# A decoder step on one core: other marks for splitting the next weights, one block's V first, three small steps moved

## The chip, the cores and the metric

The kernel runs on one core of one Trainium2 chip. The metric is the device time of one execution in microseconds (us); of the kernel before, three runs gave 1424.87 to 1428.22 us with a median of 1428.19. Every engine (TensorE, here PE; VectorE, DVE; ScalarE, ACT; GpSimd, POOL; SyncE, SP, which issues the DMAs) works through its own list of instructions in order, and the lists are tied by semaphores.

## The reference

One inference step of a hybrid decoder for 1024 prompt tokens and 8 x 8 sample tokens, 1088 tokens in all, in float32:

```python
u = rmsnorm(x)                                   # 1088 x 1024
a, q, k, v, g_a, g_b = split(u @ w_in)           # a 512, q/k/v 768 each, gates 1024 each
A = pool(a) @ w_pa                               # trailing means over 2/4/8/16 tokens
B = attention(q, k, v) @ w_pb                    # 3 head groups of 4 heads of 64; dilation 1, 4, 16
h = x + (sigmoid(g_a) * A + sigmoid(g_b) * B) @ w_o
y = h + relu(rmsnorm(h) @ w_up)**2 @ w_down      # 1024 -> 4096 -> 1024
```

q and k are RMS-normed per head. The sample tokens attend to cached keys and values as well; the caches go out shifted by eight rows.

## The kernel before

Every float32 operand of a large product is split into a high half in the type fp32r (a copy on ACT) and a low half (a subtraction on DVE), and a product is three passes: high x high, high x low, low x high. `split` (line 113) is this pair; in the trace it is lines 114 (ACT) and 115 (DVE), and lines 1279 and 1280 are the same pair in `put`. PE runs in the order of the program. On the other engines a planner, which simulates the program's timeline when it is built, sets the order. `behind_pe` makes an instruction wait until a given matmul is done.

The stages, by the trace: pooling input and row norms (to 58 us), three head groups of attention (g = 2, 1, 0, to about 395 us; the gate products begin there), gates, the two branches and `w_o` (to 741 us), the feed-forward's up product and down product.

In a head group the tokens are nine blocks: eight of 128 prompt tokens and block 8, the 64 sample tokens. Blocks 8 and 0 are done together, then 1 to 5 alone, then 6 and 7 together in groups 2 and 1. Where blocks go together, or alone at the end of group 0, the projections run as Q, K, V with 256 columns each (`qkv_part`, line 606; 24 matmuls); blocks 1 to 5 do Q and K as one product of 512 columns and V after it. After a projection the ACT squares (642), DVE `ms` (645), POOL `mr` (646) and ACT scale (651) bring Q and K to unit RMS. Block 8's two halves are first added on DVE (627, 628). A projection's result lies in one of four PSUM banks that are used in turn (`bank`), so the fifth projection after another needs that one's bank free again.

`step()` runs once for each projection (twice for the wide one). It advances every unfinished generator by one: the attention of older blocks (`attend`: transposes at 666, scores 683, row maxima 692, exp 693, transposes 702 and their copies 705, values 716, output copies 723 and 726), the pooling branch, the token sums (`token_sums`, lines 525 to 534: per step some DVE additions and products into one buffer `ts`, then its store to `ts_d`), and the sample tokens' attention (`sample_shared_keys`). `soon` puts a function into a list from which each step runs one. `own_step` advances the sample tokens' attention over their own long cache (pieces `pck` and `pcv`, multiplied on POOL at 855 and 879, reduced on DVE).

Weights of the next group: `line_up` (142) lists the twelve quarters (512 columns, which is two of the eight features panels) of the next Q, K and V weights, each with a key. They go to the places of the present Q, K and V weights. `feed` (157) splits the first of the list as soon as its key's matmul has been issued in the program, and ties the ACT half behind that matmul. The raw quarters come over three buffers (`raw`, DMAs at line 130): a quarter's load is issued when the quarter three ahead of it has been split.

The order inside one product: `gemm` (189) with `by_k=2` goes feature by feature, with all three passes of a feature panel before the next; otherwise a whole pass goes over all eight panels.

Later, in the feed-forward, `norm_sums` (1645) adds the squares of the second half of the rows with matmuls, POOL takes the power (`hr`, 1652), `norm_spread` (1655) builds diagonals on DVE (`dg`, 1657) and spreads them over partitions with four matmuls (`bc`, 1661), and `make_versions` scales the rows (1664) and forms the sums and differences which the later up products use. The up products are units of 24 matmuls; `then` hangs these functions behind chosen units.

At the switch to group 1 the pooling's memory is given back and the tiles of the new group are laid into it. `wT` (a tile of zeros to be filled later, 1142) and `osm` (1145, 1146) are cleared there.

Of the kernel before, what the change touches and what calls it, by code (L numbers as in the profile page):

```python
# [36 lines left out]
def decoder_step(ctx, tc, i, o):  # L37
# [79 lines left out]

    def split_on_vector(dst_hi, dst_lo, src):
        ins = v_.tensor_copy(dst_hi, src)
        v_.tensor_tensor(dst_lo, src, dst_hi.bitcast(F32), op=ALU.subtract)  # L120
        return ins

    def fetch(src, name, a, tied=False):
# [32 lines left out]

    def feed(splitter=split):
        while coming_up and coming_up[0]["key"] in ends_of:
            p = coming_up.pop(0)
            cs = slice(p["a"], p["a"] + 512)  # L160
            ins = splitter(p["wt"][:, 0, cs], p["wt"][:, 1, cs], p["raw"])
# [31 lines left out]

    def gemm(out, n_k, lhs, rhs, by_k=False, middle=None):

        if by_k == 2:
            terms = [(a, b, k) for k in range(n_k) for a, b in PASSES]
        elif by_k:
            terms = [(1, 0, k) for k in range(n_k)] + [(0, b, k) for k in range(n_k) for b in range(2)]
        else:  # L200
            terms = [(a, b, k) for a, b in PASSES for k in range(n_k)]
        for j, (a, b, k) in enumerate(terms):
            last_mm[0] = t_.matmul(out, lhs(a, k), rhs(b, k), start=(j == 0), stop=(j == len(terms) - 1))  # L203
            if middle and j == len(terms) // 2 - 1:
                middle()


# [397 lines left out]

    def qkv_part(g, wts, blk, name, tiles, js, middle=None):

# [13 lines left out]
        if blk == 8:  # L621
            for k in range(KD):
                t_.matmul(pt[:, :N], smp_t[:, k, :], rhs(0, k), start=(k == 0), stop=(k == KD - 1))
                if k < KD - 1:
                    for kk in ((0, 1) if k == 0 else (k + 1,)):
                        last_mm[0] = t_.matmul(pt[:n, :N], smp_t[:, kk, :NS], rhs(1, kk), start=False, stop=False)
            v_.tensor_copy(vt[:n], pt[n:, :256])
            v_.tensor_tensor(pt[:n, :256], pt[:n, :256], vt[:n], op=ALU.add)
        else:
            gemm(pt[:n, :N], KD, lambda s, k: block_cols(g, blk, s, k), rhs, g == 0 and (2 if blk == 0 and js == [2] else 1), middle)  # L630
        for j in js:
# [491 lines left out]
    for g in (2, 1, 0):  # L1123
        nq = i["qk_norm"]
        if g == 1:
# [15 lines left out]
            wT = ap2.tile([P, 2 * P], F32R, name="wT")  # L1141
            v_.tensor_scalar(wT, ident.unsqueeze(1).to_broadcast([P, 2, P]), 0.0, None, op0=ALU.mult)

            for a in range(2):
                v_.memset(osm[64:, a], 0.0)
                v_.memset(osm[64:, a, :, 64], -NEG)
            qs = sp1.tile([P, 768], F32, name="qs")
# [14 lines left out]
        for blks in ((8, 0), (1,), (2,), (3,), (4,), (5,)) + (((6, 7),) if g else ((6,), (7,))):  # L1162

            if g and 6 in blks:
                next_wts = [(place[0] + j) % 3 for j in range(3)]
                for j, after in enumerate((((7, 0), (6, 1), (6, 1), (7, 1)), ((7, 1), (6, 2), (6, 2), (6, 2)), ((7, 2),) * 4)):
                    keys_of = [(g,) + a for a in after]
                    if g == 1 and j == 2:
                        keys_of[3] = (0, 0, "mid")
                    line_up(i["w_in"][2 + 3 * j + g - 1], f"qkv{g - 1}_{j}", *keys_of)  # L1170
            elif not g and 3 in blks:
                wg_first = line_up(lambda a: gate_quarter(a // 512 % 2, a // 1024), "ga0",
                                   *((0, 7, j) for j in (0, 0, 1, 1)), width=2048)
            tiles = {b: qkv_tiles(f"{g}_{b}", b == 8) for b in blks}

            for js in (((0, 1), (2,)) if blks[0] in (1, 2, 3, 4, 5) else ((0,), (1,), (2,))):
                for b in (blks[::-1] if g == 0 and js == (2,) else blks):

# [7 lines left out]

                    def last_quarter():
                        ends_of[0, 0, "mid"] = last_mm[0]
                        feed(split_on_vector)

# [4 lines left out]
                    wide = len(js) == 2  # L1195
                    qkv_part(g, wts, b, f"{g}_{b}", tiles[b], js, middle if wide else last_quarter if (g, b, js) == (0, 0, (1,)) else None)
                    feed()
# [12 lines left out]
                    if 2 in js:  # L1210
                        (sample_block if b == 8 else prompt_block)(g, b, *tiles[b])
                if g == 2 and 2 in js and 8 in blks:
                    start(pool_branch(), "p", now=True)
                    start(token_sums(), "t", now=True)

# [695 lines left out]
    for f in range(0, FIRST, 2):  # L1911
        for n in (0, 2):
            for ff in (f, f + 1):
                groups[ff][n]()
                if f == 0:
                    then({(0, 0): lambda: norm_sums(1), (0, 1): lambda: (norm_spread(1), make_versions())}.get((n, ff), lambda: None))
    for f in range(NG):
# [260 lines left out]
```

## Time and profile before

| | |
|---|---|
| median of three runs | 1428.19 us (1424.87 to 1428.22) |
| profiled execution, its own time | 1423.59 us |
| its span, first to last instruction | 1421.8 us |
| PE busy | 1405.0 us, 99% of the span |
| DVE, ACT, POOL busy | 974.3, 755.7, 227.1 us |
| TensorE clock granted | 1.000 |

A stretch of the span is read by the busy time of each engine in it; a row of the order of time has the start, the length, the engine, the line, the operation, the tiles written and read, and in brackets the idle time before it with what ended that idle time. A row can stand for several like instructions (xcount).

### The profile page before, as it was taken

The page shows a single profiled execution, that of the slowest core. Times are in us where ns is not written, and L with a number is a line of the kernel's source. Part 1 is how long each engine was busy: PE and PEld are TensorE (multiplying, and loading weights), DVE is VectorE, ACT ScalarE, POOL GpSimd, SP SyncE. Part 2 cuts the span into 40 slices and gives each one's busy share as a digit, 9 for nine tenths or more (in the row PEclk, how much of TensorE's full clock was granted, in tenths as well). Part 3 has the DMA queues.
Part 4 walks back from the last instruction along what each step waited for, and adds up shares of the span by engine and source line. Part 5 has one row for each costly group of instructions (what it writes and reads, how often), then busy time and mean ns, then how long its engine had stood idle before and what let it go on. Part 6 is the DMA issues. An engine that isn't in the chain of part 4 may idle for free.

```text
span 1421.8 us, 29482 instructions
## 1 busy us (share of the span) xinstructions
PE 1405.0 (99%) x11101; PEld 1352.6 (95%) x11101; DVE 974.3 (69%) x1806; ACT 755.7 (53%) x1961; POOL 227.1 (16%) x291
## 2 busy tenths in 40 slices
PE   9999999999999999999999999999999999999998
PEld 8988877877999999999999999999999999999998
DVE  7688775786676776875468678765665686664565
ACT  8556755777765223563336455454554544444443
POOL 1721165565500000000000000000000000000100
PEclk9999999999999999999999999999999999999999
DMA  6323789756477777975468768856658987777674
GB/s 212 115 80 109 204 222 213 201 130 145 108 248 232 253 227 234 322 232 165 141 198 272 230 220 255 270 190 223 231 194 278 333 274 258 223 242 226 199 264 168
DMA packets 184543, 303.59 MB, mean 214 GB/s; under 512 B 26568, under 2 KB 90510, under 8 KB 182351
## 3 DMA queue, kind: packets, MB, share of 16 engines
q1 hardware_dynamic: 181326, 258.04, 58.4%
q0 software_dynamic: 3072, 43.65, 9.6%
q8 instruction: 87, 1.43, 0.4%
q14 instruction: 58, 0.47, 0.1%
HBM read 231.55 MB, written 113.73 MB: 243 GB/s over the span
## 4 chain that ended last, share of the span: by engine, by line
PE 93%; DMA 2%; ACT 2%; DVE 1%; POOL 1%; issue 0%; SPq 0%; DVEq 0%; POOLq 0%; ACTq 0%
PE pz L1272 24%; PE pd L2036 24%; PE pg L1272 12%; PE ph L203 7%; PE pqk L203 5%; PE pab L1578 5%; PE pv L203 4%; PE a L329 3%; PE pq L203 1%; PE pk L203 1%; POOL pcv L879 1%; DMA pcv<-in_cache_kv_dram 1%; PE pl L508 1%; DMA wq<-in_qk_norm_dram 0%; DMA keys<-in_kT_dram 0%; PE pog1b L716 0%
## 5 line engine op out<-in xcount | busy, mean ns | idle before, releaser
L2036 PE MATMUL pd<-places 128*128 128x272 f32 x2688 | 334.7, 287 | 0.0
L2036 PEld LDWEIGHTS pd<-places 128*128 128x128 f32 x2688 | 334.6, 188 | 0.0
L1279 ACT ACTIVATE places<-raw_d 128x544 fp32r<-128x544 f32 (+1 forms) x176 | 111.1, 647 | 163.5 <-DMA raw_d<-z_d 61.1
L1280 DVE TENSOR_TENSOR places<-raw_d,places 128x544 fp32r<-128x544 f32 (+1 forms) x176 | 122.6, 711 | 94.8 <-ACT places L1279 92.8
L2076 POOL DMA_DIRECT2D out_kv_sample_dram<-in_cache_kv_dram x96 | 47.1, 490 | 801.3 <-ACT places L1279 586.2
L1272 PE MATMUL pz<-act,places 128*128 128x272 f32 x1080 | 141.5, 289 | 0.0
L1272 PEld LDWEIGHTS pz<-act,places 128*128 128x128 f32 x1080 | 138.2, 188 | 0.0
L203 PE MATMUL ph<-act,places 128*128 128x272 f32 x768 | 97.0, 288 | 0.0
L203 PEld LDWEIGHTS ph<-act,places 128*128 128x128 f32 x768 | 96.5, 188 | 0.1
L1272 PE MATMUL pg<-act,places 128*128 128x272 f32 x576 | 76.6, 290 | 0.0
L1272 PEld LDWEIGHTS pg<-act,places 128*128 128x128 f32 x576 | 73.6, 189 | 0.6 <-issue 0.3
L646 POOL TENSOR_TENSOR mr<-ms,mhalf 128x4 f32<-128x4 f32 (+2 forms) x39 | 56.2, 1443 | 105.6 <-DVE ms L645 104.5
L1272 PE MATMUL pz<-places,apart 128*128 128x272 f32 x528 | 68.2, 287 | 0.0
L1272 PEld LDWEIGHTS pz<-places,apart 128*128 128x128 f32 x528 | 66.8, 188 | 0.0
L203 PE MATMUL pqk<-places,act 128*128 128x512 f32 x240 | 61.0, 403 | 0.7 <-ACT qk L651 0.7
L1272 PE MATMUL pz<-act,apart 128*128 128x272 f32 x456 | 59.7, 289 | 0.0
L1272 PEld LDWEIGHTS pz<-act,apart 128*128 128x128 f32 x456 | 58.3, 188 | 0.1
L203 PEld LDWEIGHTS pqk<-places,act 128*128 128x128 f32 x240 | 44.6, 192 | 10.8 <-ACT qk L651 0.9
L855 POOL TENSOR_TENSOR pck<-pck,qs 128x256 f32<-128x256 f32 x64 | 48.3, 784 | 41.2 <-DMA pck<-in_cache_kv_dram 26.8
L329 PE MATMUL a<-act,places 128*128 128x384 f32 (+1 forms) x288 | 50.3, 332 | 1.4 <-ACT act L307 1.2
L329 PEld LDWEIGHTS a<-act,places 128*128 128x128 f32 x288 | 47.5, 188 | 3.2 <-ACT act L307 1.8
L1578 PE MATMUL pab<-ab,places 128*128 128x272 f32 x384 | 50.5, 287 | 0.0
(433 smaller groups left out, 2836.1 us busy)
## 6 DMA issues: line engine op xcount, KB each, us to landing
out_kv_sample_dram<-in_cache_kv_dram POOLq DMA_DIRECT2D x72, 480.0 KB, 4.8
raw_d<-z_d SPq DMA_DIRECT2D x112, 272.0 KB
z_d<-t SPq DMA_DIRECT2D x80, 272.0 KB
raw_d<-in_w_down_dram SPq DMA_DIRECT2D x80, 256.0 KB
raw_u<-in_w_up_dram SPq DMA_DIRECT2D x64, 256.0 KB
raw_qkv<-in_w_in_dram SPq DMA_DIRECT2D x36, 256.0 KB
pck<-in_cache_kv_dram SPq DMA_DIRECT2D x32, 256.0 KB
pcv<-in_cache_kv_dram SPq DMA_DIRECT2D x32, 256.0 KB
```

What stands on the lines that cost most here:

```text
L203: last_mm[0] = t_.matmul(out, lhs(a, k), rhs(b, k), start=(j == 0), stop=(j == len(terms) - 1))
L329: last_mm[0] = t_.matmul(pts[m][:, :n], wt[:, a, kk, m * P:(m + 1) * P], act4[b][kk][:, :, part4(c)], start=(p == 0 and kk == 0), stop=(p ...
L508: t_.matmul(pl[:, :npr], lin[:, g, :], dp_[:, c0:c0 + npr], start=True, stop=True)
L646: g_.tensor_tensor(r[:n, :H], ms[:n, :H], mhalf[:n, :H], op=ALU.pow)
L855: behind_pe(g_.tensor_tensor(t[:, n], t[:, n], qs[:, :256], op=ALU.mult))
L879: behind_pe(g_.tensor_tensor(tv, tv, sc[:, j + n, :].unsqueeze(2).to_broadcast([P, 4, HD]), op=ALU.mult))
L1272: last_mm[0] = t_.matmul(x[c][:, :Q], A[:, a, k * P:(k + 1) * P], Bv(b, k, c), start=(first and n == 0), stop=(n == len(terms) - 1), skip_ ...
L1279: ins = s_.activation(view(t[:, 0]), src, AF.Copy)
L1280: v_.tensor_tensor(view(t[:, 1]), src, view(t[:, 0]).bitcast(F32), op=ALU.subtract)
L1578: last_mm[0] = t_.matmul(q[x][:, c, :Q], w.rearrange("p s n -> p (s n)")[:, at:at + P], rhs, start=(n == 0), stop=(n == len(terms) - 1))
L2036: last_mm[0] = t_.matmul(chain[t][:, c, :Q], A[:, a, t * P:(t + 1) * P], Z[:, b, c * Q:(c + 1) * Q], start=(fresh and f == 0 and n == 0), ...
L2076: ins = g_.dma_start(d, a)
```

## The change

Five parts.

1. `gemm` takes a function `quarter` and calls it after every six matmuls. In groups 2 and 1, blocks 6 and 7, Q, K and V go feature by feature (`by_k=2`), and after each six matmuls (two feature panels) a key is set and `feed` is run. The next Q's quarters are now keyed to the middle and the end of block 7's Q and the middle and the end of block 6's K; the next K's to the middle and end of block 7's K and of block 6's V; the next V's first three to the first, second and third six matmuls of block 7's V, and its last to the end of the sample block's K in the next group.
2. `split_on_vector`, which split the last quarter of group 0's V on DVE alone behind the middle of block 0's K, is gone.
3. In group 1, too, V of block 0 goes ahead of V of block 8, and V of block 0 goes feature by feature in every group.
4. In group 2 the token sums start after K of blocks 8 and 0 (before: after V). The pooling branch starts where it did.
5. The clearings of `wT` and `osm` go into the list of `soon`, behind eight empty entries, and the one of `wT` waits for PE's latest matmul. `norm_spread` and `make_versions` hang behind the third up unit instead of the second.

```diff
+            if quarter and j % 6 == 5:
+                quarter(j // 6)
...
-            gemm(pt[:n, :N], KD, lambda s, k: block_cols(g, blk, s, k), rhs, g == 0 and (2 if blk == 0 and js == [2] else 1), middle)
+            by_k = 2 if quarter or blk == 0 and js == [2] else g == 0
+            gemm(pt[:n, :N], KD, lambda s, k: block_cols(g, blk, s, k), rhs, by_k, middle, quarter)
...
-            v_.tensor_scalar(wT, ident.unsqueeze(1).to_broadcast([P, 2, P]), 0.0, None, op0=ALU.mult)
-
-            for a in range(2):
-                v_.memset(osm[64:, a], 0.0)
-                v_.memset(osm[64:, a, :, 64], -NEG)
+
+            def clear():
+                behind_pe(v_.tensor_scalar(wT, ident.unsqueeze(1).to_broadcast([P, 2, P]), 0.0, None, op0=ALU.mult))
+                for a in range(2):
+                    v_.memset(osm[64:, a], 0.0)
+                    v_.memset(osm[64:, a, :, 64], -NEG)
+
+            soon(*[lambda: None] * 8, clear)
...
-                for j, after in enumerate((((7, 0), (6, 1), (6, 1), (7, 1)), ((7, 1), (6, 2), (6, 2), (6, 2)), ((7, 2),) * 4)):
-                    keys_of = [(g,) + a for a in after]
-                    if g == 1 and j == 2:
-                        keys_of[3] = (0, 0, "mid")
+                for j, after in enumerate((((7, 0, 1), (7, 0, 3), (6, 1, 1), (6, 1, 3)), ((7, 1, 1), (7, 1, 3), (6, 2, 1), (6, 2, 3)),
+                                           ((7, 2, 0), (7, 2, 1), (7, 2, 2)))):
+                    keys_of = [(g,) + a for a in after] + [(g - 1, 8, 1)] * (j == 2)
...
-                for b in (blks[::-1] if g == 0 and js == (2,) else blks):
+                for b in (blks[::-1] if g < 2 and js == (2,) and 8 in blks else blks):
...
-                    def last_quarter():
-                        ends_of[0, 0, "mid"] = last_mm[0]
-                        feed(split_on_vector)
+                    def quarter(q):
+                        ends_of[g, b, js[0], q] = last_mm[0]
+                        feed()
...
-                    qkv_part(g, wts, b, f"{g}_{b}", tiles[b], js, middle if wide else last_quarter if (g, b, js) == (0, 0, (1,)) else None)
+                    qkv_part(g, wts, b, f"{g}_{b}", tiles[b], js, middle if wide else None,
+                             quarter if g and b in (6, 7) else None)
...
-                if g == 2 and 2 in js and 8 in blks:
-                    start(pool_branch(), "p", now=True)
-                    start(token_sums(), "t", now=True)
+                if g == 2 and 8 in blks and js != (0,):
+                    start(*((pool_branch(), "p") if 2 in js else (token_sums(), "t")), now=True)
...
-                    then({(0, 0): lambda: norm_sums(1), (0, 1): lambda: (norm_spread(1), make_versions())}.get((n, ff), lambda: None))
+                    then({(0, 0): lambda: norm_sums(1), (2, 0): lambda: (norm_spread(1), make_versions())}.get((n, ff), lambda: None))
```

More of the change, by code (lines that the diff above doesn't have):

```diff
@@ L116, in split @@
         return ins
[L118 to L121, printed above, removed]
     def fetch(src, name, a, tied=False):
@@ L155, in line_up, with feed @@
         return wt
-    def feed(splitter=split):
+    def feed():
         while coming_up and coming_up[0]["key"] in ends_of:
@@ L160, in feed @@
             cs = slice(p["a"], p["a"] + 512)
-            ins = splitter(p["wt"][:, 0, cs], p["wt"][:, 1, cs], p["raw"])
+            ins = split(p["wt"][:, 0, cs], p["wt"][:, 1, cs], p["raw"])
             behind_pe(ins, ends_of[p["key"]])
@@ L192, in behind_pe, with gemm @@
                           mybir.DependencyInfo(mybir.DependencyClass.Sync, mybir.DependencyReason.DATA), reason="pace")
-    def gemm(out, n_k, lhs, rhs, by_k=False, middle=None):
+    def gemm(out, n_k, lhs, rhs, by_k=False, middle=None, quarter=None):
         if by_k == 2:
@@ L604, in in_order, with qkv_part @@
                 nat[s, k], nat[s, k + 1] = t[:, 0, :], t[:, 1, :]
-    def qkv_part(g, wts, blk, name, tiles, js, middle=None):
+    def qkv_part(g, wts, blk, name, tiles, js, middle=None, quarter=None):
         n = min(P, TOK - blk * P)
```

## The prediction

> **What bounds the kernel now.** I read the page first, then a table by stretches, then the order of time of PE, and of the engine that released it, at each place where PE stood still.
>
> ```profile
> span 1421.8 us, 29482 instructions
> PE 1405.0 (99%) x11101; PEld 1352.6 (95%) x11101; DVE 974.3 (69%) x1806; ACT 755.7 (53%) x1961; POOL 227.1 (16%) x291
> ```
>
> PE is the bound, and the change neither adds nor removes a matmul. So it can only win what PE stands idle, 1421.8 - 1405.0 = 16.8 us, or add to it. The table by stretches (us, busy time of PE, PEld, DVE, ACT, POOL, clock, DMA share, GB/s) says where that is:
>
> ```profile
> 160.00:190.00 30.00, 25.60 (x189) 22.02 (x188) 21.91 (x75) 18.51 (x87) 9.78 (x12) 1.00 1.02 275
> 190.00:275.00 85.00, 85.00 (x759) 68.50 (x758) 57.29 (x164) 52.51 (x262) 51.40 (x61) 1.00 0.85 206
> 275.00:303.00 28.00, 25.32 (x207) 22.52 (x206) 25.32 (x54) 22.05 (x95) 17.66 (x20) 1.00 0.66 152
> 740.00:755.00 15.00, 13.23 (x104) 12.85 (x103) 8.35 (x14) 4.89 (x9) 2.98 (x5) 1.00 0.63 190
> ```
>
> 4.40 us are lost at the switch from group 2 to 1, 2.68 at the switch from 1 to 0 and 1.77 at the second norm: 8.85 of the 16.8 us. Between the switches PE loses nothing (85.00 of 85.00). The clock is 1.00 in every row. In PE's order of time the losses are these (the bracket is the idle time and its releaser):
>
> ```profile
> 173.58 0.39 PE L623 MATMUL pv<-places,smp_t 128*128 128x256 f32 x1 [1.86 <-ACT qk L651]
> ...
> 180.84 3.06 PE L203 MATMUL pqk<-places,act 128*128 128x512 f32 x12 [0.66 <-ACT qk L651]
> ...
> 186.02 0.65 PE L716 MATMUL pog2b<-pTg2b,v 128*64 128x128 f32 x6 [1.76 <-ACT pTg2b L705]
> ...
> 281.16 1.09 PE L716 MATMUL pog1b<-pTg1b,v 128*64 128x128 f32 x14 [0.25 <-ACT pTg1b L705]
> ...
> 291.43 0.38 PE L203 MATMUL pv<-places,natt 128*128 128x256 f32 x1 [0.86 <-DVE places L119]
> 292.52 0.86 PE L203 MATMUL pv<-places,natt 128*128 128x256 f32 x5 [0.70 <-DVE places L120]
> ...
> 301.00 0.65 PE L716 MATMUL pog1b<-pTg1b,v 128*64 128x128 f32 x6 [0.87 <-ACT pTg1b L705]
> ...
> 750.35 1.16 PE L1661 MATMUL bc<-dg,ones 128*128 128x272 f32 x4 [1.77 <-DVE dg L1657]
> ```
>
> Call them A, B, C (first switch), D, E (two rows, 1.56), F (second switch), G: 1.86 + 0.66 + 1.76 + 0.25 + 1.56 + 0.87 + 1.77 = 8.73 us. That is the most that the seven can return.
>
> **The change part by part.** First switch, the engines behind A to C:
>
> ```profile
> 172.10 0.63 ACT L114 ACTIVATE places<-raw_qkv 128x512 fp32r<-128x512 f32 x1 [1.42 <-DMA raw_qkv<-in_w_in_dram]
> 172.63 0.89 ACT L651 ACTIVATE qk<-pq,mr 64x64 f32<-64x64 f32 x4
> ...
> 179.88 0.91 ACT L651 ACTIVATE qk<-pk,mr 64x64 f32<-64x64 f32 x4 [2.16 <-POOL mr L646]
> 183.31 0.40 ACT L693 ACTIVATE smg2b<-smg2b,sta 128x128 f32<-128x128 f32 x1 [2.53 <-DVE sta L692]
> ```
> ```profile
> 163.00 1.36 DVE L525 TENSOR_TENSOR ts<-act,act 128x544 f32<-128x544 f32 x2 [1.08 <-DMA ts_d<-ts]
> ...
> 170.07 0.21 DVE L645 TENSOR_SCALAR ms<-ms,xeps 64x4 f32<-64x4 f32 x1
> 170.19 0.42 DVE L533 TENSOR_TENSOR ts<-ts 128x272 f32<-128x272 f32 x1
> ...
> 179.12 0.66 DVE L1142 TENSOR_SCALAR wT<-cst 128x256 fp32r<-128x256 f32 x1 [2.97 <-DMA ts_d<-ts]
> 179.88 0.56 DVE L1145 MEMSET osm<- 64x264 f32 x2
> ```
> ```profile
> 170.36 2.10 POOL L646 TENSOR_TENSOR mr<-ms,mhalf 64x4 f32<-64x4 f32 x2 [14.99 <-DVE ms L645]
> 176.76 2.13 POOL L855 TENSOR_TENSOR pck<-pck,qs 128x256 f32<-128x256 f32 x3 [4.30 <-DMA pck<-in_cache_kv_dram]
> 178.85 1.00 POOL L646 TENSOR_TENSOR mr<-ms,mhalf 64x4 f32<-64x4 f32 x1
> ```
>
> *A* is no wait for weights. PE needs the bank that block 8's Q still holds; its scale (172.63) stands on ACT behind the last quarter of V, which waited 1.42 us for its load, and its power was done only at about 171.4, since DVE gave `ms` at 170.07, between the last token sums (163.00 to 170.6). Part 4 takes the sums two projections earlier (2 x 24 matmuls at 0.12, some 6 us). Part 1 frees places up to one projection sooner, some 3 us, so that the loads, which queue in a stretch whose DMA share is 1.02, are asked for sooner and the last V quarter waits loaded. Between block 8's Q and the product that needs its bank lie three projections, some 9 us; the chain itself (`ms` 0.21, half of 2.10, the scale 0.89, and the squares and the adding, an estimate of 3 to 4 us from these) then has 5 us of cover. A goes: -1.86. If DMA stays the limit, 0; above 0 nothing speaks for it, since the chain loses work and gains none.
>
> *B* is the same chain for block 8's K, and POOL ran its power behind three multiplications that had waited for `pck` (176.76 + 2.13). PE now comes 1.86 sooner. Below: gone, -0.66; above: the scale stays where it is, +1.86. Loads come sooner but POOL's order may stand; I take +0.2.
>
> *C*: ACT stood 2.53 us for row maxima that DVE had behind the clearing of `wT`, which waited 2.97 us for the store of `ts`. Part 5 sets the clearings about nine steps later, part 4 lets the store land before; DVE gets back 2.97 + 0.66 + 0.56 = 4.2. From 0 to -1.76; I take -1.4, for what B leaves. At their later place the clearings cost 1.22 us of a DVE that is busy 57.29 of 85, in a stretch where PE loses nothing: 0 if a gap takes them, 1.2 if they stand ahead of row maxima.
>
> *V of block 0 first* (part 3, new in group 1) lets block 0's transposes come one step sooner, in the middle of the first wide product, and the sample tokens' attention one step later. The transposes need the scale of block 0's K:
>
> ```profile
> 184.46 0.89 ACT L651 ACTIVATE qk<-pk,mr 128x64 f32<-128x64 f32 x4
> ```
>
> PE is there after the product's first half, 180.84 + 3.0 = 183.8, less A and B, 181.3; if that scale stays at 185.35 the new wait is 4.1 us, if it moves with DVE (4.2 us regained) it is 0. I take +0.6. The V product itself keeps its 24 matmuls; by features it costs nothing, and for group 2's first V there is no wait to win.
>
> Second switch:
>
> ```profile
> 280.00 0.63 ACT L114 ACTIVATE places<-raw_qkv 128x512 fp32r<-128x512 f32 x1 [0.91 <-DMA raw_qkv<-in_w_in_dram]
> ...
> 298.78 0.93 ACT L651 ACTIVATE qk<-pk,mr 128x64 f32<-128x64 f32 x4 [1.33 <-POOL mr L646]
> ```
> ```profile
> 285.28 3.14 PE L203 MATMUL pk<-places,natt 128*128 128x256 f32 x24
> ```
> ```profile
> 290.96 0.42 DVE L119 CAST places<-raw_qkv 128x512 fp32r<-128x512 f32 x1
> ```
>
> *E*: the last quarter was split on DVE at 290.96, late behind the softmax of the sample tokens. Now its high half goes to ACT (0.63) and its mark, the end of block 8's K, lies before 285.28 instead of at the middle of block 0's K (285.28 + 1.5 = 286.8); only the subtraction stays on DVE. PE needs the quarter at 291.43 - 0.86 = 290.6. The cover is 5.3 us less 0.63 and a subtraction (0.69 in the row of 748.78 below), 4 us: -1.56, from 0; DVE loses the cast's 0.42, ACT gains 0.63. *D* was ACT held for a load (0.91): -0.25, from 0. *F*: ACT waits 1.33 for POOL's power, then PE for ACT. PE arrives 1.8 sooner on a chain of nearly full engines (DVE 25.32 of 28): from -0.87 to +1.8; I take +0.5. The sample attention's later step frees the memory of `natt` one projection later:
>
> ```profile
> 267.83 2.36 ACT L602 CAST natt<-act 128x256 fp32r<-128x256 f32 x4
> ...
> 277.42 3.12 PE L203 MATMUL pq<-places,natt 128*128 128x256 f32 x24
> ```
>
> The casts would come one projection later, about 3.5 us, and end at 273.7 against 277.42; set behind ACT's other work up to the split at 280.00, they would end at 280.6. From 0 to +3.2; nearer the first, since PE's need comes first in the program: +0.4.
>
> *G*, the second norm:
>
> ```profile
> 745.65 1.99 POOL L1652 TENSOR_TENSOR hr<-hms,mhalf 128x4 f32<-128x4 f32 x2 [0.28 <-DVE hms L1651]
> 748.78 0.69 DVE L1280 TENSOR_TENSOR places<-raw_uf,places 128x512 fp32r<-128x512 f32 x1 [2.57 <-ACT places L1279]
> 749.39 0.82 DVE L1657 TENSOR_TENSOR dg<-cst,hr 128x640 f32<-128x640 f32 x1
> ```
>
> The third unit's 24 matmuls, about 3.0 us, now run while POOL and DVE work: PE reaches `bc` at 751.4, and `dg` is done at 750.2. -1.77; 0 if the planner sets `dg` behind the next unit's split again, which waits for PE. The sums after it come 2.9 us later against PE. Their cover is long:
>
> ```profile
> 786.24 1.28 DVE L115 TENSOR_TENSOR t<-y,t 128x1088 fp32r<-128x1088 f32 x1
> ...
> 805.65 3.15 PE L1272 MATMUL pz<-t,places 128*128 128x272 f32 x24
> ```
>
> 18 us from write to use; nothing.
>
> Sum: -1.86 + 0.2 - 1.4 + 0.6 - 0.25 - 1.56 + 0.5 + 0.4 - 1.77 = -5.14 us. The profiled execution took 1423.59 (span 1421.8 and 1.8 around it), 4.6 under the median, so it would be 1418.4; on the median, 1428.19 - 5.1 = **1423.0**.
>
> **Rivals.** *Clean* (R1): all seven go and nothing new comes: -8.7, so 1419.5. For it: every wait has its own part; against it: B and F hang on POOL, which no part relieves.
>
> *Marks hold ACT* (R2, no change). More splits now wait for a matmul, and what stands behind them waits too. The trace shows the kind:
>
> ```profile
> 748.12 0.63 ACT L1279 ACTIVATE places<-raw_uf 128x512 fp32r<-128x512 f32 x1 [3.03 <-PE pz L1272]
> 748.65 0.59 ACT L1823 COPY t_e<-pz 128x544 f32<-128x544 f32 x1
> ```
>
> A mark twelve matmuls ahead holds ACT 12 x 0.12 = 1.4 us; where ACT already decides (B, C, F) three such holds give 4.3 back: -0.8, so 1427.4. Against it: before, ACT waited for loads at these places anyway. [...]
>
> *The new order starves PE* (R3, slower). V of block 0 first asks ACT and POOL for block 0's scale and for `natt` at the moment when both are late already. The transposes wait their 4.1 and C stays behind them, so the first switch changes by -4.28 + 4.1 + 1.76 = +1.6; in the second `natt` costs its 3.2 and F its 1.8 against D's and E's 1.8, +3.2. With G gone the sum is +3.0, 1431.2; where the planner leaves `dg` late too, +4.8, 1433.0. It decides from a `natt` wait above some 2 us on. For it: the casts take 2.36 of an ACT that is busy 22.05 of 28; against it: they have 7 us from the freed memory (one projection after 267) to PE's need at 277.42.
>
> *Nothing moves* (R4): the planner, which orders ACT and DVE by its own clock, puts the splits and the clearing where they were, and only G goes: 1426.4.
>
> **How the numbers follow.** My sum or near it (-3 to -7): 0.47. R1: 0.17. R2 and R4 together: 0.20. R3: 0.16. About 0.3%, 4.3 us, is what a measurement of this kernel can tell from no change. Faster by more: R1 and some six sevenths of the first case, 0.57. Slower by more: two thirds of R3, 0.11. The same: 0.32, with R2, R4 and what is left of the first case and of R3. The range goes from R1 less most of what the lowest run lies under the median (1428.19 - 1424.87 = 3.3), 1417, to 1430, just short of R3; R3 and a little at the lower end, not 2 in 10, lie outside.
>
> **What would show it.** Right: idle PE in 160 to 190 under 2 us, no wait for DVE at block 0's V in group 0 (lines 119 and 120 are gone), no idle before `bc`; ACT's waits for `raw_qkv` fewer. Wrong: PE waiting at `tqg1b` for ACT, at the first `pq<-places,natt` for ACT, or ACT waiting for PE at its split lines around 140 to 160 and 255 to 280.

## The result, and the profile after

The changed kernel takes 1421.89 us (median of 13 runs, 1417.64 to 1425.92); the kernel before, run beside it, 1426.31 (13 runs, 1423.65 to 1429.40). The ratio is 0.9968 with a 95% interval of 0.9957 to 0.998: 4.4 us or 0.32% less. The forecast was 1423.0.

The profile needs a caution first. It is one execution, and that of the changed kernel took 1424.17, 2.3 us above its median, while that of the kernel before took 1423.59, 2.7 below its own. So the two spans are almost equal, although the kernels are not. In the changed kernel most of the program's lines carry numbers two to five smaller than before (the scale is 649 instead of 651, the products' matmul 198 instead of 203). The page of the changed kernel (span, busy times):

```profile
span 1422.4 us, 29497 instructions
PE 1406.4 (99%) x11101; PEld 1354.8 (95%) x11101; DVE 971.3 (68%) x1805; ACT 755.0 (53%) x1962; POOL 221.7 (16%) x291
```

The table by stretches (us; busy time of PE, PEld, DVE, ACT, POOL; clock, DMA share, GB/s), at the places the prediction used:

```profile
160.00:190.00 30.00, 29.68 (x236) 26.66 (x235) 17.92 (x55) 16.95 (x85) 10.02 (x12) 1.00 1.00 264
190.00:275.00 85.00, 78.25 (x671) 62.04 (x668) 52.47 (x166) 46.29 (x244) 48.42 (x60) 0.98 0.79 194
275.00:303.00 28.00, 28.00 (x247) 25.64 (x247) 23.58 (x64) 25.19 (x105) 16.98 (x22) 1.00 0.55 148
...
740.00:755.00 15.00, 15.00 (x119) 14.81 (x119) 5.78 (x11) 5.20 (x10) 3.32 (x5) 1.00 0.49 152
```

The three places lost 8.85 us before; they now lose 0.32. The loss has moved: between the switches, where PE had lost nothing, it stands idle for 6.75 us, and the clock is 0.98. In PE's order of time:

```profile
181.80 0.65 PE L714 MATMUL pog2b<-pTg2b,v 128*64 128x128 f32 x6 [0.32 <-ACT pTg2b L703]
195.56 0.44 PE L957 MATMUL pss<-kt,qS 128*32 128x136 f32 x8 [1.63 <-DVE keys L922]
...
210.27 0.65 PE L714 MATMUL pog1b<-pTg1b,v 128*64 128x128 f32 x6 [1.82 <-ACT pTg1b L703]
215.93 0.44 PE L957 MATMUL pss<-kt,qS 128*32 128x136 f32 x8 [0.91 <-DVE p L959]
...
270.38 0.37 PE L681 MATMUL sg1b<-qkTg1b,qkTg1b 64*128 64x128 f32 x1 [1.47 <-ACT pTg1b L703]
```

181.80 is what is left of C. The next three are the sample tokens' scores (`pss`) and the first attention of group 1; the last stands just ahead of the second switch. What ACT, DVE and SP did ahead of the first (three excerpts of the order of time):

```profile
191.06 0.22 ACT L640 ACTIVATE qk<-pqk 128x64 f32<-128x64 f32 x1 [4.39 <-DMA out_kv_sample_dram<-qk]
...
192.64 0.57 ACT L666 ACTIVATE qkn<-tqs,wqs 128x64 f32<-128x64 f32 x2
```
```profile
192.84 0.27 DVE L643 TENSOR_SCALAR ms<-ms,xeps 128x8 f32<-128x8 f32 x1 [8.46 <-ACT qk L640]
193.04 1.13 DVE L928 COPY qS<-qkn 64x8 f32<-64x8 f32 x3
...
195.31 0.81 DVE L922 COPY kt<-qkn 128x32 f32<-128x32 f32 x1
```
```profile
183.83 16.19 SPq L838 DMA_DIRECT2D pck<-in_cache_kv_dram  x4
...
202.61 0.50 SPq L913 DMA_DIRECT2D kt<-in_kT_dram  x1
```

The squares of the first wide product are written over the sample tokens' Q and K, whose keys were still on their way out to memory: ACT waited 4.39 us for that store. Behind the squares stood the scale of the sample tokens' transposes (`qkn`), and DVE stood 8.46 us for the squares themselves, ahead of the copies into `qS`, `kt` and `keys` that PE needs. SP came through four loads of the own keys (`pck`) only in 16 us. In the kernel before, `qkn` ran ahead of the squares, these waited for PE and not for the store, and SP was through the same four loads in 3.87 us (ACT, then SP, before):

```profile
187.46 0.52 ACT L668 ACTIVATE qkn<-tqs,wqs 128x64 f32<-128x64 f32 x2
190.50 0.22 ACT L642 ACTIVATE qk<-pqk 128x64 f32<-128x64 f32 x1 [2.52 <-PE pqk L203]
```
```profile
185.53 3.87 SPq L840 DMA_DIRECT2D pck<-in_cache_kv_dram  x4
```

The last loss, 1.47 us at 270.38, is of another kind: the copy that PE waited for stood behind a split that had waited for its load (ACT in the changed kernel):

```profile
267.81 0.63 ACT L114 ACTIVATE places<-raw_qkv 128x512 fp32r<-128x512 f32 x1 [3.79 <-DMA raw_qkv<-in_w_in_dram]
...
269.91 0.42 ACT L703 COPY pTg1b<-tpg1b 128x256 f32<-128x256 f32 x1
```

### The profile page after: what moved, and what is told of

Same layout as the page of the kernel before. It is cut to its first block, busy times and chain, and to the rows that moved or that the text cites. A ratio compares the mean times of both kernels' runs of the same rounds, so it can differ in the third digit from the quotient of the medians.

```text
span 1422.4 us, 29497 instructions
## 1 busy us (share of the span) xinstructions
PE 1406.4 (99%) x11101; PEld 1354.8 (95%) x11101; DVE 971.3 (68%) x1805; ACT 755.0 (53%) x1962; POOL 221.7 (16%) x291
## 4 chain that ended last, share of the span: by engine, by line
PE 84%; DMA 5%; DVE 5%; ACT 2%; POOL 2%; issue 1%; SPq 0%; DVEq 0%; POOLq 0%; ACTq 0%
PE pz L1272 24%; PE pd L2036 24%; PE pg L1272 11%; PE ph L198 7%; PE pab L1578 5%; PE a L326 3%; PE pqk L198 3%; PE pv L198 2%; DMA ts_d<-ts 1%; DMA pcv<-in_cache_kv_dram 1%; POOL pck L853 1%; DMA raw_qkv<-in_w_in_dram 1%; PE pq L198 1%; DMA out_kv_sample_dram<-qk 1%; ACT qk L640 1%
## 5 line engine op out<-in xcount | busy, mean ns | idle before, releaser
L644 POOL TENSOR_TENSOR mr<-ms,mhalf 128x4 f32<-128x4 f32 (+2 forms) x39 | 50.9, 1307 | 106.0 <-DVE ms L643 105.7
L198 PE MATMUL pv<-places,act 128*128 128x256 f32 x384 | 51.3, 291 | 0.0
```

What stands on the lines that cost most here:

```text
L644: g_.tensor_tensor(r[:n, :H], ms[:n, :H], mhalf[:n, :H], op=ALU.pow)
```

## The experiments

All against the kernel before on the same chip (us; medians; ratio with its 95% interval):

| run | what it is | this | before | ratio |
|---|---|---|---|---|
| e1_again | the changed kernel again | 1421.03 | 1425.56 | 0.9968 [0.9957, 0.9979] |
| e2_early_store | changed, one store sooner | 1419.93 | 1425.56 | 0.9962 [0.9948, 0.9975] |
| e3_v8_first | changed, old order of V in group 1 | 1418.83 | 1425.56 | 0.9954 [0.9942, 0.9967] |
| e4_norm_only | before + 5b | 1424.43 | 1425.56 | 0.9988 [0.9978, 0.9998] |
| e5_quarters_only | before + 1, 2 | 1426.10 | 1426.01 | 1.0000 [0.9990, 1.0010] |
| e6_order_only | before + 3 | 1426.82 | 1426.01 | 1.0003 [0.9990, 1.0017] |
| e7_sums_only | before + 4 | 1422.71 | 1426.01 | 0.9981 [0.9971, 0.9991] |
| e8_sums_clear | before + 4, 5a | 1420.84 | 1426.01 | 0.9965 [0.9953, 0.9977] |
| e9_sums_clear_norm | before + 4, 5a, 5b | 1420.24 | 1426.45 | 0.9956 [0.9944, 0.9967] |
| e10_quarters_first | e3, quarters at the first switch alone | 1418.95 | 1426.45 | 0.9948 [0.9936, 0.9960] |
| e11_last_mark | e3, no quarters but the last mark | 1418.38 | 1426.45 | 0.9942 [0.9930, 0.9954] |
| e12_power_first | e11, one step of own keys moved | 1418.66 | 1426.18 | 0.9948 [0.9934, 0.9962] |

**Do the new losses recur?** The changed kernel, unaltered.

> The changed kernel itself, once more, beside the three others on one chip. Its first profile shows 6.75 us of idle PE between 190 and 275 us, where the kernel before has none, and it shows 4.39 us in which ACT waited (at 191.06, the squares of the first wide product of group 1) for the store of the sample tokens' keys. Theory S (store): that wait is built into the new order of times: PE comes to the wide product some 4 us sooner, the store does not land sooner, and what stands behind it (DVE 8.46 us, the cached keys' loads on SP, the next keys) comes late. Then the idle time of 4 to 7 us shows again in 190 to 275, and the time is 1421 to 1423. Theory O (order): the losses come because V of block 0 now runs ahead of V of the sample tokens, so that their attention starts a projection later; the same numbers. Theory C (chance): this one execution had a late transfer; then 190 to 275 shows PE busy for 84 to 85 of its 85 us in this profile, and the median is still about 1422.

They do: PE is busy for 80.66 us of 190 to 275, ACT waits 3.49 us for the store, and PE loses 0.72 and 2.92 us at `pss`. Theory C falls; between S and O this run can't choose.

**The store, or the order?** First the store alone, sooner by its place in the program:

```diff
+                    if g < 2 and b == 8 and 1 in js:
+                        soon(lambda dst=rows[:, :256], src=tiles[8][0][:64, 256:]: behind_pe(dma_st(dst, src)))
...
-        for dst, src in ((rows[:, :256], qk[:64, 256:]), (rows[:, 256:], vt[:64])) + (
+        for dst, src in (((rows[:, :256], qk[:64, 256:]),) if g == 2 else ()) + ((rows[:, 256:], vt[:64]),) + (
```

> The changed kernel, with one store issued sooner: in groups 1 and 0 the sample tokens' keys go out right behind their scale and weights (178.2 us in the profile) and not behind V of the sample tokens (182.26). Nothing else moves. Theory S: ACT no longer waits for that store at the first wide product of group 1 (4.39 us to 0), DVE's 8.46 us of waiting shrink by as much, the idle PE time in 190 to 275 falls from 6.75 to under 2 us, and the time is 3 to 5 us under that of the changed kernel: 1417 to 1419. Theory O: the sample tokens' attention is as late as before, the idle time stays at 4 to 7 us and the time at 1421 to 1423. Theory C: no difference in time, and no idle time in either.

Then the order alone:

```diff
-                for b in (blks[::-1] if g < 2 and js == (2,) and 8 in blks else blks):
+                for b in (blks[::-1] if g == 0 and js == (2,) and 8 in blks else blks):
```

> The changed kernel, with V of the sample tokens first again in group 1 (block 0's second), as before the change; group 0 keeps its order. Theory S: the store of the sample tokens' keys is issued one step (about 3 us) sooner, the wait of 4.39 us goes or nearly, and the idle time in 190 to 275 falls under 2 us; the transposes of block 0 come later again; time 1418 to 1420. Theory O: the same idle time gone, the same time, and the tables of these two theories differ only in the run with the early store. If the new order of V is itself worth what it was made for, the time is above that of the changed kernel by up to 2 us (1424); theory C: within 1 us of the changed kernel.

With the store sooner, ACT's wait falls from 4.39 to 1.57 us, but PE still loses at the sample scores (PE in the run with the early store):

```profile
195.72 0.44 PE L957 MATMUL pss<-kt,qS 128*32 128x136 f32 x8 [0.16 <-DVE keys L922]
...
215.35 0.44 PE L957 MATMUL pss<-kt,qS 128*32 128x136 f32 x8 [2.10 <-DVE p L959]
```

With the old order the wait for the store is still there, and costs nothing (ACT in the run with V of the sample tokens first):

```profile
183.30 0.52 ACT L666 ACTIVATE qkn<-tqs,wqs 128x64 f32<-128x64 f32 x2
187.20 0.23 ACT L640 ACTIVATE qk<-pqk 128x64 f32<-128x64 f32 x1 [3.38 <-DMA out_kv_sample_dram<-qk]
```

`qkn` is done before the wait and not behind it; PE loses nothing ahead of 207.55, and there 0.61. So theory S in its simple form falls: the wait for the store costs only what the order puts behind it. The three profiles with the new order in a kernel with the sums sooner lose at `pss`, and none with the old order does. In time e3 is 2.2 us under e1; their intervals overlap (0.9942 to 0.9967 against 0.9957 to 0.9979), so the size is less sure than the place. The early store's 1.1 us is not told from nothing.

**The second norm alone.** The one entry `(0, 1)` of the last loop becomes `(2, 0)` in the kernel before.

> The kernel before, with nothing but the spread of the second norm moved two units later. By the sum's term G the 1.77 us of idle PE ahead of bc go and nothing comes in their place: 1.8 us under the kernel before, so 1424.5 against 1426.3, a ratio of 0.9988. By the rival in which the planner leaves dg late, the idle time before bc stays above 1 us and the time is that of the kernel before.

The idle time ahead of `bc` is gone:

```profile
740.00:755.00 15.00, 15.00 (x123) 14.97 (x122) 5.62 (x10) 4.75 (x9) 2.96 (x4) 1.00 0.48 148
```

The medians are 1.1 us apart; the ratio is 0.9988 as expected (1.7 us), and its interval reaches from 0.3 to 3.1 us and holds the 1.77.

**Each other part alone**, in the kernel before, with the lines of the change's diff that belong to it: the marks by quarter and the last split on ACT (e5), the order of V with its products by feature (e6), `token_sums()` started two products sooner (e7), and this with `clear()` put off (e8).

> The kernel before with parts 1 and 2 alone: the splits of the next weights marked behind quarters of the matmuls, and no half mark and no split on DVE for the last one; the order of V, the token sums, the clearing and the norm as before. By my sum's terms D, E and F: E's 1.56 and D's 0.25 go, F gives between 0.87 won and 1.8 lost. Theory L (A hangs on the load of the last V quarter): A's 1.86 goes too, and the time is about 3.5 us under the kernel before. Theory P (A hangs on DVE, which gives ms only behind the token sums): A stays, and the time is about 1.5 us under it. By the rival that marks hold ACT: no gain, or up to 2 us slower, with ACT waiting for PE at its split lines.

> The kernel before with part 3 alone: V of block 0 ahead of V of the sample tokens in group 1 too, and by feature in groups 2 and 1. The run with V of the sample tokens first was 2.2 us under the changed kernel. Theory O2 (the order itself costs): with A to C standing, PE waits at the transposes of block 0 (up to 4.1 us), or at the first sample scores between 193 and 216 us (1 to 3 us); time 1 to 4 us above the kernel before. Theory S2 (it costs only where PE has come sooner through A to C): A to C stand here, so PE comes late enough; nothing between 193 and 216 and a time within 1 us of the kernel before.

> The kernel before with part 4 alone: the token sums begun one projection pair sooner; the clearing stays where it was. By theory P: A's 1.86 goes and B's 0.66 goes or stays; C's 1.76 falls, since the store of the sums has landed when the clearing needs it; 2 to 4 us under the kernel before. By theory L: A and B stay (the last V quarter's load is as late), C falls alone, 0.5 to 1.8 us.

> The kernel before with part 4 and the later clearing (5a). Against the run with the sums alone it tells what the clearing's place is worth once the sums are sooner: by my sum the store's landing was the wait (2.97 of 4.2 us), so the difference is 0 to 0.7 us. If C hangs on the clearing itself, C goes here and not in the run with the sums alone, 1.4 us.

The quarters alone win nothing in time. All of A and C to F go, but at both switches PE loses the time again in one longer wait (the first switch: PE, DVE, ACT; then the second: PE, ACT; in the run with the quarters alone):

```profile
182.78 3.78 PE L198 MATMUL pqk<-places,act 128*128 128x512 f32 x8 [4.70 <-ACT qk L649]
```
```profile
176.88 0.86 DVE L1141 TENSOR_SCALAR wT<-cst 128x256 fp32r<-128x256 f32 x1 [2.44 <-DMA ts_d<-ts]
```
```profile
181.05 0.40 ACT L691 ACTIVATE smg2b<-smg2b,sta 128x128 f32<-128x128 f32 x1 [5.11 <-DVE sta L690]
```
```profile
277.22 1.03 PE L714 MATMUL pog1b<-pTg1b,v 128*64 128x128 f32 x6 [3.39 <-ACT pTg1b L703]
```
```profile
271.51 0.63 ACT L114 ACTIVATE places<-raw_qkv 128x512 fp32r<-128x512 f32 x1 [2.12 <-DMA raw_qkv<-in_w_in_dram]
273.37 0.63 ACT L114 ACTIVATE places<-raw_qkv 128x512 fp32r<-128x512 f32 x1 [1.23 <-DMA raw_qkv<-in_w_in_dram]
274.69 2.20 ACT L599 CAST natt<-act 128x256 fp32r<-128x256 f32 x4
276.79 0.38 ACT L703 COPY pTg1b<-tpg1b 128x256 f32<-128x256 f32 x1
```

At the first switch PE comes sooner to a DVE that still waits for the store of the sums (2.44 us) with the clearing; the row maxima come late behind it, ACT stands 5.11 us for them ahead of the scale of block 8's K, and B grows from 0.66 to 4.70. At the second, the splits come sooner in ACT's order than their loads in time: two waits for `raw_qkv` (2.12 and 1.23 us), then the casts of `natt` (2.20), and only then the copy that PE waits for, 3.39 us. Before, the same casts and the same copy ended at 270.5 and cost nothing.

The order alone costs PE the wait at block 0's transposes that the prediction had named, since A to C stand (the run with the order alone):

```profile
186.32 0.44 PE L666 MATMUL tqg1b<-cst,qk 128*128 128x128 f32 x2 [0.43 <-DVE sta L692]
187.84 0.73 PE L666 MATMUL tqg1b<-cst,qk 128*128 128x128 f32 x2 [1.08 <-ACT qk L651]
```

Nothing is lost between 193 and 216 there, and in time it isn't told from the kernel before. That fits theory S2; the wait at the transposes, 1.5 us in all, is O2's sign, and A stands with 2.19 us. Sums alone: A and C are gone and B is 1.40. With the clearing later, B is 2.27, and the time 1420.84; the difference of 1.9 us to the sums alone is at the edge of what these runs can tell, and no wait in the two profiles explains it; the mean clock lost differs by 0.9 us (last section).

**Do the parts add?** The kernel before with 4, 5a and 5b.

> The kernel before with parts 4, 5a and 5b: sums sooner, clearing and norm later; the marks of the splits and the order of V as before. If the parts add, it is 5.2 + 1.1 = 6.3 us under the kernel before (1419.7 against 1426.0), and so 2 us under the whole change: the marks and the order of V together would then cost the whole change about 2 us. If the marks are worth something that only shows once the sums are sooner (B, 2.47 us, stands in the run with sums and clearing), it is no better than the whole change (1421 to 1422).

They do, within what the intervals can tell: 0.9956, where the two parts make 0.9965 x 0.9988 = 0.9953. It is not slower than the whole change (0.9968): the marks and the order of V, taken together, were worth nothing or cost a little.

**The stall at 268 to 277.** From e3, quarter marks at the first switch only (the other switch by whole products, its last mark kept behind block 8's K):

```diff
-                                           ((7, 2, 0), (7, 2, 1), (7, 2, 2)))):
+                                           ((7, 2, 0), (7, 2, 1), (7, 2, 2))) if g == 2 else
+                                          (((7, 0), (6, 1), (6, 1), (7, 1)), ((7, 1), (6, 2), (6, 2), (6, 2)), ((7, 2),) * 3)):
...
-                             quarter if g and b in (6, 7) else None)
+                             quarter if g == 2 and b in (6, 7) else None)
```

> The changed kernel with V of the sample tokens first in group 1, and with the quarter marks at the first switch alone: from group 1 to group 0 the splits are marked behind whole products as before, only the last quarter of V stays behind block 8's K and on ACT. Theory H (at the second switch the splits, set sooner, hold ACT for loads that do not come sooner, so that pTg1b and natt come late and PE loses 3.4 us at about 268): that wait goes, 190 to 275 shows PE busy for 84 of 85 us or more, E and D stay won, and the time is 2 to 4 us under the run with V of the sample tokens first, 1415 to 1417. Theory M (the stall at 268 has another cause, as natt's memory coming free late): it stays, and the time is 1418 to 1420.

Then at neither switch (`quarter` is None everywhere, the same marks for group 2 with (2, 7, 2) last). Against e9 this adds only the last quarter's mark and its split on ACT at the second switch, and V of block 0 by feature in groups 2 and 1:

> As the run before it, but with no quarter marks at all: whole-product marks at both switches, the last quarter of V at the second switch behind block 8's K and on ACT. Against the run before it tells what quarters at the first switch are worth: B (1.6 to 2.5 us idle ahead of the first wide product, in the runs with the sums sooner) should be back if the quarters removed it, and the time 1 to 3 us above; if B goes with the sums and the clearing alone, no difference.

Theory H is right about the place. The stall (3.36 us in e3) is gone (the run with quarters at the first switch alone, stretches and PE):

```profile
190.00:275.00 85.00, 84.83 (x752) 67.99 (x751) 55.88 (x165) 53.05 (x261) 51.95 (x62) 1.00 0.86 207
275.00:303.00 28.00, 26.07 (x206) 22.78 (x204) 24.97 (x54) 21.48 (x91) 18.55 (x24) 1.00 0.60 158
```
```profile
289.40 0.86 PE L198 MATMUL pv<-places,natt 128*128 128x256 f32 x5 [0.89 <-DVE places L115]
297.78 0.65 PE L714 MATMUL pog1b<-pTg1b,v 128*64 128x128 f32 x6 [0.77 <-ACT pTg1b L703]
```

It is wrong about the price: the 2 to 4 us expected below e3 aren't there, the two can't be told apart (0.9948 and 0.9954). Half of E (0.89) and F (0.77) are back. Without any quarters the time is the same again (0.9942), although B is back there with 2.57 us. This version has the lowest ratio of the study; its interval (0.9930 to 0.9954) lies below that of the changed kernel (0.9957 to 0.9979), by a little, and as the lowest of twelve it may owe a part to chance.

**B by itself.** In e11, POOL and PE around B (`ms` was done at 174.68; the power that reads it came behind three multiplications that stood for their load):

```profile
176.50 2.11 POOL L853 TENSOR_TENSOR pck<-pck,qs 128x256 f32<-128x256 f32 x3 [5.94 <-DMA pck<-in_cache_kv_dram]
178.56 1.00 POOL L644 TENSOR_TENSOR mr<-ms,mhalf 64x4 f32<-64x4 f32 x1
```
```profile
180.56 3.06 PE L198 MATMUL pqk<-places,act 128*128 128x512 f32 x12 [2.57 <-ACT qk L649]
```

```diff
-                        (1, 7, (1,)), (1, 6, (2,)), (1, 7, (2,)), (0, 7, (1,)), (0, 7, (2,)))
+                        (1, 0, (1,)), (1, 7, (1,)), (1, 6, (2,)), (1, 7, (2,)), (0, 7, (2,)))
```

> The run with whole-product marks and the last mark alone (1418.4), and one step of the own keys' work taken from behind block 0's K in group 1 (its three pck multiplications stood on POOL ahead of the power for block 8's K, and waited 5.94 us for their load, until 176.50) and given to block 7's K in group 0. Theory Q (B is POOL's order: ms was there at 174.68, the power came at 178.56): the power comes before 176, the 2.57 us of idle PE ahead of the first wide product go or fall under 1 us, and the time is 0 to 2.5 us less, 1416 to 1418.4; 0 if what comes next on ACT (C) takes it, as in the run with quarters at the first switch, where B was gone and the time the same. Theory N (the power is late for another reason, or the moved step costs the same elsewhere): B stays, or 1419 to 1421 from a later step.

Theory Q holds: the power comes at 174.71, ahead of the multiplications, and PE is never idle in the first switch (POOL, the stretch, and PE, in this run):

```profile
174.71 1.00 POOL L644 TENSOR_TENSOR mr<-ms,mhalf 64x4 f32<-64x4 f32 x1 [3.10 <-DVE ms L643]
176.28 1.01 POOL L644 TENSOR_TENSOR mr<-ms,mhalf 128x4 f32<-128x4 f32 x1 [0.57 <-DVE ms L643]
178.52 5.82 POOL L853 TENSOR_TENSOR pck<-pck,qs 128x256 f32<-128x256 f32 x8 [1.23 <-DVE qs L848]
```
```profile
160.00:190.00 30.00, 30.00 (x252) 26.80 (x251) 19.11 (x68) 20.72 (x107) 11.81 (x14) 1.00 0.92 256
```
```profile
286.08 4.21 PE L198 MATMUL pv<-places,natt 128*128 128x256 f32 x18 [2.80 <-ACT qk L649]
```

PE keeps its lead for 100 us, and gives it back at the second switch in the same form: there POOL's power for block 8's Q stands behind `pck` multiplications that waited 7.08 us for their load. The time can't be told from e11's (0.9948 and 0.9942). By these two profiles the 2.57 us moved from one switch to the other; the step was not tried with the same done there.

## Why the prediction was right, and where it was wrong

The time was right (1423.0 forecast, 1421.89 measured; 5.1 us less forecast, 4.4 measured). The working was right about the seven places, but that the sum came out is in part luck: it left out a loss elsewhere, and it left out the clock.

*The seven places.* By the profile, A 1.86, B 0.66, D 0.25, E 1.56, F 0.87 and G 1.77 went entirely and C fell from 1.76 to 0.32: 8.4 us. That is rival R1's sum, not mine. But 6.75 us came back between the switches. In e1's profile the switches and the norm still lose 2.16 us and the stretch between them 4.34. So where the kernel before loses 8.85 us the changed kernel loses 7.07 and 6.50: only 1.8 and 2.4 us of idle time are won, not the 5.1 of the sum. R1's gains came together with losses in a place that no rival named.

- *A* (-1.86) and its reason, DVE and loads both: the sums alone removed it, and so did the quarters alone. My either-or was right to take it whole, but what a part wins here depends on B: with the quarters alone B grew by 4.04 us, more than A and C had given (3.62).
- *B* (+0.2; ends -0.66 and +1.86): 0 in the changed kernel, and 1.40 to 2.71 with the sums and without the quarters, beyond the upper end of 2.52 (0.66 + 1.86) in two profiles. That POOL's order decides was right, as the last run shows.
- *C* (-1.4): 0.32 left in one profile of the changed kernel, 1.69 in the other. The term is the right size for the first alone.
- *The transposes' wait* (+0.6; ends 0 and 4.1): none in the changed kernel, 0.43 and 1.08 where the order stood alone. That the scale moves with DVE, the condition of the lower end, came out. The upper end's (A and B gone, the scale unmoved) was met by no run: with the order alone A stood.
- *D, E* (-1.81): gone (of D 0.40 stands in e1's profile). The cover named for E held, but the price was not looked for in the right place.
- *F* (+0.5): -0.87 instead. PE had lost time before it; where it had not, in the run with quarters at the first switch alone, F stands with 0.77.
- *natt* (+0.4): no wait at Q in group 0, 0.27 and 0.56 us at that group's first wide product in the two profiles. The casts did cost, but as work ahead of `pTg1b` on ACT, in the run with V of the sample tokens first and in that with the quarters alone.
- *G* (-1.77): gone; alone 1.1 us by the medians and 1.7 by the ratio, with 1.77 inside the interval.

*The clock.* "The clock is 1.00 in every row" held for the one profile of before, and the prediction left the clock out. The record has the granted clock of every run. In e1 the 21 runs of the kernel before lost 2.6 us to it on average, the 10 of the changed kernel 0.3. The mean times (1425.8 and 1421.0) are 4.8 us apart; an estimate from the last section's 0.8 us of time for each us lost is that some 2 us of the gain are clock that is no longer lost, and some 3 idle time. So waits, of which the prediction's sum is made, gave only a part of what it got right.

*The steps that failed* are two. The first: "the sample tokens' attention one step later" was costed by `natt`'s memory alone. It should have been followed down ACT and DVE: the scale of those transposes went behind the squares of the next product, which waited 4.39 us for a store, and PE then lost 1.63 and 0.91 us at the sample scores (0.72 and 2.92 in e1). In the profile of before no row shows that wait; that PE came later there than the store's landing fits the run with the order alone, where A stands and nothing is lost at the scores. The second: marks by quarter were taken to bring the loads sooner, so that ACT's waits for `raw_qkv` become fewer. At the first switch they did (5.0 us before, 2.7 after, between 160 and 215 us). At the second switch they became longer. ACT's waits for `raw_qkv` between 250 and 285 us sum to 3.3 us before, 4.4 with the quarters alone and 5.3 in the changed kernel. (In e1's profile PE loses nothing there, busy for 16.00 of the 16 us from 264 to 280: in the changed kernel this loss comes and goes.) The splits moved sooner in ACT's order; the loads did not keep up. In both profiles the next load went out after DVE's half of the split, not after ACT's: in the changed kernel ACT's half of the first of these quarters began at 257.41 (before 259.63), but DVE's at 260.86 (before 260.30), behind a sum over `pck` that had stood 2.37 us for POOL. So the next load went out no sooner, at 261.57 (before 261.02; SP, before and after), and ACT stood 3.79 us for it:

```profile
261.02 0.35 SPq L130 DMA_DIRECT2D raw_qkv<-in_w_in_dram  x1
```
```profile
261.57 0.94 SPq L125 DMA_DIRECT2D raw_qkv<-in_w_in_dram  x2
```

*The rivals.* R2's form (ACT is held by its splits) is what happened at the second switch, but by loads, not by marks: waits for PE at the split line were at most 0.5 us there. The rows show what the copy of `pTg1b` stood behind: in the changed kernel (269.91) a split that had waited 3.79 us for its load, with the quarters alone (276.79) splits that had waited 2.12 and 1.23 us and casts of 2.20 us. R3 named the right part (V of block 0 first) and the wrong waits. R4 falls: splits, clearing and norm all moved.

The sentence "Between the switches PE loses nothing" was read as safety. It was cover that the change used up: PE's early arrival was worth only what the engines behind it allowed.

## What to carry to other kernels

When several waits on one path are removed, look up what each later consumer waits for *now less the lead you give it*: the store that frees `qk` (4.39 us of ACT after) and the load of a quarter (3.79 us of ACT after) cost PE, which came later before, nothing between the switches (85.00 of 85.00 us), and the power behind multiplications 0.66 us at the first (2.57 in e11). A step moved later must be followed through what stands behind it on each engine, not only to its own consumer (here `qkn`, behind squares that waited 4.39 us on ACT, and the copies behind it on DVE, which stood 8.46 us), and a split marked sooner was worth nothing where its load did not come sooner; it only held ACT, here for those 3.79 us. Where a change bundles parts, measure them alone: here two parts (sums and clearing) with the norm carry the whole gain in time, and the marks and the order of V together gave none. And read the clock of many runs, not of one profile, before a gain is put down to waits.

## What the runs showed of the hardware

*A stall of PE sometimes cost more than its length.* With 11 of the 28 over 1.2 us the clock granted fell to 0.50 for some us; such a dip began between 1.0 us before the stall's end and 1.2 us after it (the table by microseconds for e3, whose stall of 3.36 us ended at 271.65):

```profile
269.00:270.00 1.00, 0.00 (x0) 0.00 (x0) 1.00 (x5) 1.00 (x5) 0.02 (x1) 1.00 1.08 236
270.00:271.00 1.00, 0.00 (x0) 0.00 (x0) 1.00 (x7) 1.00 (x3) 0.72 (x1) 0.81 1.13 270
271.00:272.00 1.00, 0.35 (x4) 0.35 (x5) 1.00 (x5) 1.00 (x5) 0.29 (x1) 0.50 0.72 209
...
277.00:278.00 1.00, 1.00 (x9) 1.00 (x9) 0.00 (x0) 0.51 (x2) 0.00 (x0) 0.78 0.60 170
278.00:279.00 1.00, 1.00 (x11) 1.00 (x10) 0.97 (x3) 1.00 (x3) 0.00 (x0) 1.00 0.33 109
```

The 28 are all such stalls after the first 20 us, in the 14 profiles. Of the 10 that lasted 2.1 us or more, 8 had such a dip; of the 18 between 1.2 and 1.9 us, 3 (1.47, 1.76 and 1.77 us). Between the first 20 us and the end of PE's work no dip came without a stall; a twelfth followed two of 0.43 and 1.08 us within 2 us, in the run with the order alone. The lost clock, summed, was 1.70 to 1.72 us in eight dips and 3.40 to 3.42 in four, nothing between; the second kind is the one above, with 0.50 from 271 to 277 and a part of the microsecond on either side (0.81 and 0.78). The same stall (C, 1.76 us) had no dip in the kernel before and 3.41 us in the run with the norm alone. So the prediction's 8.73 us of idle time was not quite "the most that the seven can return": the three long ones (A, C, G) had no dip there, but A had one of 1.70 us in the run with the order alone (2.19 us long there) and G one of 1.71 in that with the sums alone. What makes a dip follow one stall and not another, no run shows.

*The clock of the runs.* The clock that a run lost is one less its mean granted clock, times its span; on record it is rounded to steps of 1.4 us, so only means over many runs say something. Over the 76 runs of the kernel before beside the experiments it is 2.8 us, and the time rises by 0.8 us with each us of it (a straight line through the 76). The changed kernel's 23 runs lost 1.3 (the first 13) and 0.3 us (e1); the quarters alone 4.9, the order alone 1.7, the sums alone 1.9, with the clearing 1.0, with the norm too 1.2; e3 2.3, e10 0.0, e11 0.7 and e12 1.9. The quarters alone lost 2.0 us more clock than the kernel before beside them (2.9) in the same time, so something else in them should have been won; their profile, the longest of their runs, doesn't show what, and it stays open. No run held the clock fixed, so how a gain divides between idle time and clock is an estimate throughout.

*The profiled execution was the longest of its runs in 8 of the 12 experiments* (e1 to e6, e8, e11), by up to 2.5 us over the next. Stalls and dips read from such a profile are then probably more than the typical run has; between e3 and e10 the profiled times differ by 2.0 us (1421.22 and 1419.22) and the medians by 0.1.
